# One transformer layer with a mixture of experts on one core: weight pieces on multiples of 512 bytes, two changes of PSUM banks, and a ring of 20 pieces in place of 19

## The chip, the core and the metric

The kernel runs on one core of a Trainium2 chip. The core has a matrix engine (TensorE, PE in the profile), whose matmuls write into 8 banks of PSUM; VectorE (DVE), ScalarE (ACT), GpSimd (POOL) and SyncE (SP), whose queue issues all the transfers here; and 16 DMA engines that bring data from the chip's memory (HBM) into the core's own (SBUF, 128 partitions). The metric is the time of one execution in microseconds. All data are float32.

## What is computed

The reference is one layer for 256 tokens of width 1024: a mixer (differential attention and a gated linear recurrence side by side, from one input projection), and then a mixture of 32 experts of which each token takes 4. Cut to the part that takes most of the time:

```python
def moe(h, router_w, router_b, w_gate_up, b_gate_up, w_down, b_down):
    logits = xf @ router_w + router_b               # 256 tokens x 32 experts
    top_v, top_i = lax.top_k(logits, 4)
    gates = jax.nn.softmax(top_v, axis=-1)
    ...                                             # for the tokens of each expert e:
        gu = xb @ w_gate_up[e] + b_gate_up[e]       # 1024 -> 2 x 1024
        g, u = jnp.split(gu, 2, axis=-1)
        g = jnp.minimum(g, 7.0); u = jnp.clip(u, -7.0, 7.0)
        y = ((u + 1.0) * (g * jax.nn.sigmoid(1.702 * g))) @ w_down[e] + b_down[e]
    ...                                             # out[token] += gate * y
```

An expert has 12 MB (12 x 1.049 MB) of weights; the 32 of them are 403 MB of the 462 MB that the kernel reads.

## The kernel before

**Pieces and the ring.** Weights lie in pieces of 128 partitions x 2048 float32 (8 KB of a partition, 1 MB in all). `piece(i)` (L72) gives piece i: 16 (`NA`) from the pool `arena`, which also serve the mixer, and 3 (`NM`) from the pool `mo`, which takes the room of the mixer's pool `late` after the mixer. In the experts the pieces form a ring, `slots`: `spot()` turns it by one, and `chunk()` (L84, its DMA is L87) loads into the piece that it gives. An expert loads eight pieces of `w_gate_up` (128 rows of 2048 each, an 8 KB row to a partition) and four of `w_down` (two rows of 4 KB to a partition). A load waits until PE has read what lay in its piece before, one whole turn of the ring ago. All loads go through SP's queue in order.

**Pools in SBUF.** `const` lies first, then `arena`, then `small`; `mo` and `late` are laid out from the other end. Where a piece starts follows from the sizes of the tiles that stand before it. Before the change the arena's pieces start 32 bytes past a multiple of 512, the three of `mo` 480 bytes past one.

**Experts.** The loop at L1131 runs over 32 experts in order; their token counts are read into registers, and `tc.If` picks code by the count. An expert with up to 32 tokens runs blocks of 32 (`gate_up_32` L948, `down_32` L975), with 33 to 64 tokens a block of 64 (`gate_up_64` L937, `down_64` L967), and with 65 to 96 both: a block of 64 and one of 32 for the rest (`so`, `gdo`), first the one of 32 and then the one of 64. More than 96 tokens take `rare` (L1072) and `rest_of` (L1026), after the loop's last loads. On PE the order of an expert is: the gate and up matmuls (in two halves of four pieces), a filler (`fill`: the matmuls that gather the tokens of the next pair of experts, `gather` L907), and then `out_of` (L1017) once or twice: `transposed` (L958) turns the activations, `turned` (L992) the combine weights, the down matmuls run over four pieces, ACT copies the result to `y`, and `combine` (L997) multiplies by the weights into four PSUM tiles that DVE adds to `acc` (L1007). Experts go in pairs (`EB` = 2): `gather_batch` (L917) makes one-hot columns on DVE (`onehot`, L892) and then the gathers.

**Banks.** PSUM has the pools `psa` (4 banks), `psb` (2) and `psc` (2); each call of `bank` takes the pool's next one in turn. An expert takes three of `psa` (`pg`, `pu`, `po`). Each `out_of` takes from `psb`: half of the transposes, the down result, two tiles of `combine`; and from `psc`: the other half of the transposes, the bank of `turned`, the other two tiles of `combine`. `gather` takes from `psc`. In `combine` the order of the four tiles is 0, 1, 2, 3 for a block of 32; tiles 0 and 1 are in `psc`, 2 and 3 in `psb`, and DVE adds in the same order.

## Time and profile before

| | us |
|---|---|
| median of three runs (1241.19 to 1246.12) | 1243.11 |
| the profiled execution | 1242.41 |
| its span, first to last instruction | 1240.4 |
| PE busy in the span | 1009.2 (81%) |
| DVE, ACT, POOL busy | 430.8, 227.7, 26.6 |

The profile is one execution of the kernel, recorded instruction by instruction. Its numbers are us from the first instruction on; it has views of busy time by line, of who waited for whom, of stretches of the span ("windows") and of instructions in order of time. "issue" as what ended a wait means that the engine waited for nothing that the profile shows; "PEq" is PE's sequencer; "SPq" is the queue of SyncE, which issues the loads. "PEclk" is the granted clock of TensorE, 1.00 being 2.4 GHz and 0.50 being 1.2 GHz. The DMA engines' mean over the span is 375 GB/s. The mixer takes about the first 270 us, the experts the rest.

### The profile page before, as it was taken

The page shows a single profiled execution, that of the slowest core. Times are in us where ns is not written, and L with a number is a line of the kernel's source. Part 1 is how long each engine was busy: PE and PEld are TensorE (multiplying, and loading weights), DVE is VectorE, ACT ScalarE, POOL GpSimd, SP SyncE. Part 2 cuts the span into 40 slices and gives each one's busy share as a digit, 9 for nine tenths or more (in the row PEclk, how much of TensorE's full clock was granted, in tenths as well). Part 3 has the DMA queues.
Part 4 walks back from the last instruction along what each step waited for, and adds up shares of the span by engine and source line. Part 5 has one row for each costly group of instructions (what it writes and reads, how often), then busy time and mean ns, then how long its engine had stood idle before and what let it go on. Part 6 is the DMA issues. An engine that isn't in the chain of part 4 may idle for free. (4 is left out here: it accounts for less than half of the span.)

```text
span 1240.4 us, 17345 instructions
## 1 busy us (share of the span) xinstructions
PE 1009.2 (81%) x6774; PEld 520.6 (42%) x6774; DVE 430.8 (35%) x843; ACT 227.7 (18%) x426; POOL 26.6 (2%) x36
## 2 busy tenths in 40 slices
PE   6999999998779899888799789668776667787845
PEld 3767777864433333433344333223332222333312
DVE  3498779642222222322222232212222212121212
ACT  3544656331111000100001110000100000010001
POOL 1020100010000000000000000000000000000000
PEclk9999989989999999999999999889989887888978
DMA  9967669879999999799999999999999999999994
GB/s 343 337 242 280 204 215 352 320 319 397 411 413 415 413 415 414 316 391 388 415 413 414 414 413 413 413 415 416 414 413 413 415 412 414 407 407 408 413 411 180
DMA packets 100191, 465.70 MB, mean 375 GB/s; under 512 B 9716, under 2 KB 9814, under 8 KB 67256
## 3 DMA queue, kind: packets, MB, share of 16 engines
q1 hardware_dynamic: 100024, 463.31, 93.7%
q8 instruction: 125, 2.05, 0.7%
q14 instruction: 42, 0.34, 0.1%
HBM read 462.23 MB, written 1.05 MB: 373 GB/s over the span
## 5 line engine op out<-in xcount | busy, mean ns | idle before, releaser
L955 PE MATMUL bank<-piece,xg 128*32 128x512 f32 x1472 | 209.7, 684 | 66.7 <-DMA piece<-in_w_gate_up_dram 54.8
L945 PE MATMUL bank<-piece,xg 128*64 128x512 f32 x768 | 170.7, 596 | 3.6 <-PEq L1155 2.7
L1007 DVE TENSOR_TENSOR acc<-acc,bank 128x512 f32<-128x512 f32 x136 | 84.4, 682 | 249.2 <-PE bank L1004 249.2
L923 DVE TENSOR_SCALAR bank<-bank 128x256 f32<-128x256 f32 (+1 forms) x35 | 18.3, 524 | 373.4 <-PE bank L955 260.4
L955 PEld LDWEIGHTS bank<-piece,xg 128*32 128x32 f32 x1472 | 43.8, 117 | 207.7 <-DMA piece<-in_w_gate_up_dram 123.8
L980 PE MATMUL bank<-piece,actT 128*32 128x256 f32 x1472 | 99.3, 421 | 6.0 <-DMA piece<-in_w_down_dram 2.7
L924 ACT ACTIVATE s<-bank 128x256 f32<-128x256 f32 (+1 forms) x32 | 14.8, 463 | 480.0 <-DVE bank L923 480.0
L945 PEld LDWEIGHTS bank<-piece,xg 128*64 128x64 f32 x768 | 56.1, 138 | 111.5 <-issue 100.5
L913 PEld LDWEIGHTS bank<-oh,x 128*128 128x128 f32 x512 | 87.7, 203 | 31.7 <-issue 22.0
L913 PE MATMUL bank<-oh,x 128*128 128x192 f32 (+1 forms) x512 | 96.8, 346 | 0.4 <-DVE xg L905 0.4
L972 PE MATMUL bank<-piece,actT 128*64 128x512 f32 x384 | 86.5, 604 | 0.8
L130 PE MATMUL bank<-lo,piece 128*128 128x512 f32 x208 | 84.1, 404 | 3.3 <-DVE lo L122 3.3
L131 PE MATMUL bank<-hi,piece 128*128 128x512 f32 x208 | 83.9, 403 | 0.0
L129 PE MATMUL bank<-hi,piece 128*128 128x512 f32 x208 | 82.6, 402 | 0.0
L122 DVE TENSOR_TENSOR lo<-piece,hi 128x1024 fp32r<-128x1024 f32 x60 | 74.0, 1254 | 16.7 <-ACT hi L121 16.5
L980 PEld LDWEIGHTS bank<-piece,actT 128*32 128x32 f32 x1472 | 49.3, 120 | 50.7 <-issue 18.3
L121 ACT CAST hi<-piece 128x1024 fp32r<-128x1024 f32 x60 | 62.0, 1047 | 45.0 <-PE bank L131 36.7
L964 PE MATMUL bank<-ident,s 128*128 128x128 f32 x88 | 17.0, 299 | 63.1 <-DVEq L1188 29.1
L1004 PE MATMUL bank<-y,gt 32*128 32x256 f32 (+1 forms) x544 | 49.2, 396 | 21.0 <-ACT y L1023 21.0
L1004 PEld LDWEIGHTS bank<-y,gt 32*128 32x128 f32 (+1 forms) x544 | 33.4, 185 | 44.2 <-ACT y L1023 42.1
L972 PEld LDWEIGHTS bank<-piece,actT 128*64 128x64 f32 x384 | 26.8, 139 | 52.8 <-issue 48.0
L1023 ACT COPY y<-bank 128x256 f32<-128x256 f32 (+1 forms) x35 | 15.6, 445 | 179.4 <-PE bank L980 96.9
(265 smaller groups left out, 875.2 us busy)
## 6 DMA issues: line engine op xcount, KB each, us to landing
piece<-in_w_gate_up_dram SPq DMA_DIRECT2D x256, 1024.0 KB, 20.2
piece<-in_w_down_dram SPq DMA_DIRECT2D x128, 1024.0 KB, 20.3
piece<-in_w_in_dram SPq DMA_DIRECT2D x22, 1024.0 KB, 6.6
piece<-in_w_mod_dram SPq DMA_DIRECT2D x16, 1024.0 KB, 8.3
piece<-in_w_mod_dram SPq DMA_DIRECT2D x16, 512.0 KB, 7.0
piece<-in_w_out_dram SPq DMA_DIRECT2D x4, 1024.0 KB, 5.1
piece<-in_w_branch_a_dram SPq DMA_DIRECT2D x2, 1024.0 KB, 8.0
piece<-in_w_branch_b_dram SPq DMA_DIRECT2D x2, 1024.0 KB, 7.5
```

Source lines behind the costliest of these rows:

```text
L121: now(A, lambda: nc.scalar.copy(hi, v[:, h]))
L122: now(V, lambda: nc.vector.tensor_tensor(lo, v[:, h], hi.bitcast(F32), ALU.subtract))
L129: nc.tensor.matmul(out, ah, bh, start=start, stop=False, skip_group_check=True)
L130: nc.tensor.matmul(out, ah, bl, start=False, stop=False, skip_group_check=True)
L131: return nc.tensor.matmul(out, al, bh, start=False, stop=stop, skip_group_check=True)
L913: last = nc.tensor.matmul(ph[:, j], x[:, t, k * P : (k + 1) * P], oh[:, t, cs], start=t == 0, stop=t == NT - 1)
L945: nc.tensor.matmul(pp[r : r + C], xg[:, k, :C], wg[k][:, 0, 512 * q : 512 * (q + 1)], start=False, stop=k == KD - 1, skip_group_check=True)
L955: nc.tensor.matmul(halves(po[U * q : U * q + U]), xg[:, k, s0 : s0 + U], quarter(wg[k][:, 0], q), start=False, stop=k == KD - 1, skip_grou ...
L972: nc.tensor.matmul(py[C * n : C * n + C], at[:, j, C * half : C * half + C], wd[kk // 2][:, kk % 2, 512 * n : 512 * (n + 1)], start=kk == ...
L980: nc.tensor.matmul(py[U * c : U * c + U, 0:256], at[:, j, U * q : U * q + U], wd[kk // 2][:, kk % 2, 256 * c : 256 * (c + 1)], start=kk == ...
L1004: nc.tensor.matmul(pcs[c][:, t], gt[r : r + n, t * P : (t + 1) * P], y[r : r + n, w : w + 256], start=True, stop=True)
L1007: nc.vector.tensor_tensor(acc[:, :, cs], acc[:, :, cs], pcs[c], ALU.add)
```

## The change

- `NM` goes from 3 to 4: a fourth piece in `mo`, the ring has 20.
- Room for it: one buffer in place of two for the one-hot tile `oh`; the tile `y` goes (the down result is copied into `so` or into the activations' own tile); `w2` lies in a buffer of `xg` and is made as the filler of expert 30, no longer at expert 27; `xr` of the overflow path lies in a ring piece.
- Places: `iota` has 128 columns in place of 352, `r2` is padded to 96 columns and `gt` by 120, so that all pieces, of the arena and of `mo`, start at multiples of 512 bytes. The overflow path compares with shifted positions (`moved`), since `iota` is shorter.
- Banks: `turned` gets a bank of `psa` in every expert (`pt`), no longer one of `psc`; `combine` of a block of 32 takes its tiles in the order 2, 0, 3, 1.

```diff
--- before.py
+++ after.py
@@ -40,7 +40,7 @@
 EB = 2
 BIG = 3.0e38
 NA = 16
-NM = 3
+NM = 4
 LASTS = 27
 NOSYNC = mybir.DependencyInfo(mybir.DependencyClass.NoSync, mybir.DependencyReason.DATA)
 NEG = float(np.finfo(np.float32).min)
@@ -169,11 +169,11 @@
     lower = late.tile([P, P], F32, name="lower")
     nc.gpsimd.affine_select(out=lower, in_=ones, pattern=[[1, P]], compare_op=ALU.is_gt, fill=0.0,
                             base=0, channel_multiplier=-1)
-    iota = const.tile([P, S + CA], F32, name="iota")
-    nc.gpsimd.iota(iota, pattern=[[1, S + CA]], base=1, channel_multiplier=0, allow_small_or_imprecise_dtypes=True)
+    iota = const.tile([P, P], F32, name="iota")
+    nc.gpsimd.iota(iota, pattern=[[1, P]], base=1, channel_multiplier=0, allow_small_or_imprecise_dtypes=True)
 
     xn2 = part(11, 0, NT, D)
-    r2 = const.tile([P, NT], F32, name="r2")
+    r2 = const.tile([P, 96], F32, name="r2")[:, :NT]
     acc = const.tile([P, NT, D], F32, name="acc")
     gw2 = const.tile([P, KD], F32, name="gw2")
     s2 = late.tile([P, D], F32, name="s2")
@@ -893,7 +893,7 @@
         return last
 
     def onehot(e0, ne, s0, n):
-        oh = mo.tile([P, NT, EB, CA], F32, name="oh")
+        oh = mo.tile([P, NT, EB, CA], F32, name="oh", bufs=1)
         oh = oh.rearrange("p t e c -> p t (e c)")[:, :, : ne * n].rearrange("p t (e c) -> p t e c", c=n)
         for t in range(NT):
             slot_is(oh[:, t], t, e0, ne, s0, n)
@@ -997,7 +997,7 @@
     def combine(gt, y, n):
 
         pcs = [bank((psc, psb)[c // 2], NT, 256) for c in range(4)]
-        order = range(4) if n == U else (0, 2, 1, 3)
+        order = (2, 0, 3, 1) if n == U else (0, 2, 1, 3)
         for t in range(NT):
             for c in order:
                 r, w = (U * c, 0) if n == U else (C * (c // 2), 256 * (c % 2))
@@ -1017,15 +1017,16 @@
     def out_of(at, wd, n, y, gd, gt, fin, pt):
 
         py = bank(psb)
-        turned(gd, gt, bank(psc) if pt is None else pt)
+        turned(gd, gt, pt)
         (down_64 if n == C else down_32)(at, wd, py)
         w = 512 if n == C else 256
         nc.scalar.copy(y[:, :w], py[:, :w])
         combine(gt, y, n) if fin is None else combine_into(fin, gt, y, n)
 
-    def rest_of(e, s0, xr, spare):
-
-        ring = deque(spare[1:])
+    def rest_of(e, s0, spare):
+
+        ring = deque(spare[2:])
+        xr = part(piece(spare[1]), 0, KD, P)
 
         def half(w, kh, n):
 
@@ -1034,7 +1035,11 @@
             nc.sync.dma_start(v, rows(a[w][e], 512 * kh, 4)[:, :, 512 * n : 512 * (n + 1)])
             return v
 
-        oh = onehot(e, 1, s0, P)
+        moved = small.tile([P, NT], F32, name="moved")
+        nc.vector.tensor_scalar(moved, posm[:, :, e], float(-s0), None, ALU.add)
+        oh = mo.tile([P, NT, P], F32, name="oh", bufs=1)
+        for t in range(NT):
+            nc.vector.tensor_scalar(oh[:, t], iota, moved[:, t : t + 1], r2[:, t : t + 1], ALU.is_equal, ALU.mult)
         for kp in range(KD // 2):
             gather(oh, xr, kp, pool=psb)
         p = piece(spare[0])
@@ -1049,11 +1054,11 @@
                     for k in range(4):
                         nc.tensor.matmul(pp[i], xr[:, 4 * kh + k, :P], w[:, k], start=False, stop=kh == 1 and k == 3)
             transposed(swiglu(*pp, s), at[:, h], 4)
-        gd = mo.tile([P, 512], F32, name="y", bufs=1)
+        gd = mo.tile([P, 512], F32, name="s", bufs=1)
         pt = bank(psb, S)
         for t in range(NT):
             gv = gd[:, t * P : (t + 1) * P]
-            weigh(gv.unsqueeze(1), e, t, s0)
+            nc.vector.tensor_scalar(gv, iota, moved[:, t : t + 1], gates[:, t, e : e + 1], ALU.is_equal, ALU.mult)
             nc.tensor.transpose(pt[:, t * P : (t + 1) * P], gv, ident)
         nc.scalar.copy(gt, pt)
         for n in range(2):
@@ -1073,19 +1078,18 @@
 
         engines = [ET.PE, ET.Activation, ET.DVE, ET.SP]
         of = lambda i: nc.values_load(counts[0:1, i : i + 1], engines=engines, min_val=0, max_val=S)
-        xr = mo.tile([P, KD, EB * CA], F32, name="xg")
         with tc.If(of(NE) > CA) as some:
             for e in range(NE):
                 cnt = of(e)
                 with tc.If(cnt > CA):
-                    rest_of(e, CA, xr, spare)
+                    rest_of(e, CA, spare)
                     with tc.If(cnt > CA + P):
-                        rest_of(e, CA + P, xr, spare)
+                        rest_of(e, CA + P, spare)
         return some
 
 
     xg = mo.tile([P, KD, EB * CA], F32, name="xg")
-    oh = mo.tile([P, NT, EB, CA], F32, name="oh")
+    oh = mo.tile([P, NT, EB, CA], F32, name="oh", bufs=1)
     for t in range(NT):
         seq(V, lambda: slot_is(oh[:, t], t, 0, EB, 0, CA))
     count()
@@ -1127,7 +1131,7 @@
 
     down_loads = lambda e: [chunk(rows(a["w_down"][e], 2 * P * i, 2), 2, D) for i in range(4)]
     after = load(0)
-    fin = pt = other = None
+    fin = other = None
     for e in range(NE):
         j = e % EB
         cnt = after
@@ -1135,13 +1139,17 @@
         if e == NE - 1:
             wd = down_loads(e)
             step(rare(list(slots)[: len(slots) - KD - 4]).cond_inst)
-        if e == LASTS:
-            w2 = mo.tile([P, D], F32, name="w2", bufs=1)
-            for n, pr in enumerate(rows_of(gw2, psc)):
-                nc.scalar.copy(w2[:, 512 * n : 512 * (n + 1)], pr)
         if j == 0:
             xgn, todo = gather_batch(e + EB) if e + EB < NE else (None, [])
             fill = first if e == 0 else todo[:2]
+            if e == NE - 2:
+                w2 = mo.tile([P, KD, EB * CA], F32, name="xg").rearrange("p a b -> p (a b)")[:, :D]
+
+                def gated_rows():
+                    for n, pr in enumerate(rows_of(gw2, psc)):
+                        nc.scalar.copy(w2[:, 512 * n : 512 * (n + 1)], pr)
+
+                fill = [gated_rows]
         elif e < NE - 1:
             fill = todo[0 if e == 1 else 2 :] + (down_bias() if e == LASTS else [])
         xe = xg[:, :, j * CA : (j + 1) * CA]
@@ -1182,25 +1190,26 @@
             after = in_turn(lambda: load(e + 1))
             wd = down_loads(e)
         else:
-            pt, other = bank(psa), bank(psa)
+            other = bank(psa)
+        pt = bank(psa)
         at = mo.tile([P, 4, P], F32, name="actT", bufs=1)
-        y, gt = mo.tile([P, 512], F32, name="y", bufs=1), mo.tile([P, S], F32, name="gt", bufs=1)
+        gt = mo.tile([P, S + 120], F32, name="gt", bufs=1)[:, :S]
         with tc.If(cnt > C) as more:
             transposed(so, at[:, 0:2], 2, other)
-            out_of(at[:, 0:2], wd, U, y, gdo, gt, fin, pt)
+            out_of(at[:, 0:2], wd, U, so, gdo, gt, fin, pt)
         step(more.cond_inst)
         with tc.If(cnt > U) as many:
             transposed(act, at, 4, other)
-            out_of(at, wd, C, y, gd, gt, fin, pt)
+            out_of(at, wd, C, act, gd, gt, fin, pt)
         with many.Else():
             transposed(act[:, :256], at[:, 0:2], 2, other)
-            out_of(at[:, 0:2], wd, U, y, gd, gt, fin, pt)
+            out_of(at[:, 0:2], wd, U, act, gd, gt, fin, pt)
         step(many.cond_inst)
         if j == EB - 1:
             xg = xgn
 
 
-    sq = mo.tile([P, NT, 256], BF16, name="fsq", tag="oh")
+    sq = mo.tile([P, NT, 256], BF16, name="fsq", tag="oh", bufs=1)
     ss = small.tile([P, NT, 4], F32, name="fss")
 
     def squares(t, c):
```

## Rows read from the trace of the kernel before

**Rows 1.** the page's slices of the span: GB/s moved in 40 equal slices

```profile
GB/s 343 337 242 280 204 215 352 320 319 397 411 413 415 413 415 414 316 391 388 415 413 414 414 413 413 413 415 416 414 413 413 415 412 414 407 407 408 413 411 180
```

**Rows 2.** waits of the queue that issues loads, whole span: us, times, longest

```profile
SPq L87 <- DMA piece<-in_w_gate_up_dram: 238.1, 133, 3.1
SPq L87 <- DMA piece<-in_w_down_dram: 187.3, 93, 3.0
```

**Rows 3.** DMA issues: name, count, KB each, median us to landing

```profile
piece<-in_w_gate_up_dram SPq DMA_DIRECT2D x256, 1024.0 KB, 20.2
piece<-in_w_out_dram SPq DMA_DIRECT2D x4, 1024.0 KB, 5.1
x<-in_x_dram SPq DMA_DIRECT2D x1, 1024.0 KB, 5.0
```

**Rows 4.** windows: us, busy by engine, PEclk, DMA share, GB/s

```profile
271.00:560.00 289.00, 246.94 (x1680) 108.98 (x1684) 78.32 (x168) 30.94 (x69) 0.00 (x0) 0.98 0.98 396
560.00:1226.00 666.00, 508.95 (x3786) 214.05 (x3782) 156.15 (x340) 58.98 (x140) 0.00 (x0) 0.90 1.01 408
```

**Rows 5.** waits of PE, 271 to 560 us: us, times, longest

```profile
PE bank L964 <- issue: 8.9, 2, 5.0
PE bank L935 <- issue: 4.1, 1, 4.1
PE bank L994 <- DVE xg L905: 2.2, 2, 1.2
PE bank L955 <- DMA piece<-in_w_gate_up_dram: 0.5, 1, 0.5
```

**Rows 6.** waits of PE, 560 to 1230 us

```profile
PE bank L955 <- DMA piece<-in_w_gate_up_dram: 54.3, 50, 2.2
PE bank L964 <- issue: 18.3, 5, 4.8
```

**Rows 7.** windows of 10 us

```profile
260.00:270.00 10.00, 9.14 (x44) 9.00 (x44) 4.44 (x27) 1.79 (x5) 1.80 (x1) 0.50 1.01 421
510.00:520.00 10.00, 7.48 (x48) 3.28 (x50) 2.91 (x5) 1.10 (x3) 0.00 (x0) 1.00 0.42 161
520.00:530.00 10.00, 8.85 (x52) 3.75 (x50) 3.08 (x6) 0.58 (x1) 0.00 (x0) 1.00 0.93 359
560.00:570.00 10.00, 9.49 (x70) 2.78 (x63) 0.43 (x1) 0.32 (x1) 0.00 (x0) 0.81 0.92 329
```

**Rows 8.** waits of the queue in 508 to 535, then 552 to 568 us

```profile
SPq L87 <- PE bank L972: 18.3, 4, 14.4
SPq L87 <- PE bank L955: 12.7, 5, 8.8
```

**Rows 9.** timeline, two experts with over 64 tokens: start, us, engine, line

```profile
459.16 0.26 ACT L965 COPY actT<-bank 128x128 f32<-128x128 f32 x1
459.92 0.41 PE L994 MATMUL bank<-ident,gdo 128*128 128x128 f32 x2 [0.99 <-DVE xg L905]
465.63 2.48 DVE L1007 TENSOR_TENSOR acc<-acc,bank 128x512 f32<-128x512 f32 x4 [5.66 <-PE bank L1004]
467.66 0.63 PE L964 MATMUL bank<-ident,s 128*128 128x128 f32 x4 [2.05 <-DVE acc L1007]
468.61 8.55 PE L972 MATMUL bank<-piece,actT 128*64 128x512 f32 x32
...
514.52 7.09 PE L972 MATMUL bank<-piece,actT 128*64 128x512 f32 x32
```

**Rows 10.** window in the first of these experts

```profile
468.00:472.00 4.00, 4.00 (x15) 1.44 (x15) 0.53 (x2) 0.74 (x2) 0.00 (x0) 0.57 1.03 413
```

**Rows 11.** timeline of PE: first matmuls of two experts

```profile
558.60 0.62 PE L935 MATMUL bank<-bgu,sel 96*32 96x512 bf16 x4 [4.14 <-issue]
...
1208.25 0.62 PE L935 MATMUL bank<-bgu,sel 96*32 96x512 bf16 x4 [6.68 <-PEq L1155]
```

**Rows 12.** groups of instructions by line: count, busy us, mean ns, idle before

```profile
L892 DVE TENSOR_SCALAR oh<-iota,posm,r 128x96 f32<-128x96 f32 x64 | 18.1, 324 | 3.7 <-PE bank L913 2.0 <-DVE xg L905 0.8
```

## The prediction, made before the result was known

> **What bounds the kernel now.** I read the slices of the span first: the DMA engines move 407 to 416 GB/s nearly everywhere after the first quarter, with one hole near 500 to 560 us [rows 1]. The queue that issues the loads mostly waits for earlier loads: 238.1 and 187.3 us [rows 2]. A load of 1024 KB (1.049 MB) takes 1.049/0.413 = 2.54 us of transfer and lands 20.2 us after its issue [rows 3], so some eight are under way at a time; a deeper ring does not make the transfer itself quicker.
>
> Then I split the expert stage in two, because the hole does. From 271 to 560 us PE is busy 246.94 of 289 us and the rate is 396; from 560 to 1226 us PE is busy 508.95 of 666 and the rate is 408 [rows 4]. PE's own waits say the same more sharply. In the first stretch it waited for a load 0.5 us in all; the rest is its own idle time ("issue"), DVE's banks and ACT [rows 5]. In the second it waited 54.3 us for loads [rows 6]. So **PE sets the time up to about 560 us, and the loads set it from there to the end.** The places where the loads stood still are 510 to 530 and 560 to 570 us: against 414 GB/s the three windows shown lose (414-161)/41.4 = 6.1, 1.3 and 2.1 us, 9.5 us together [rows 7]. There the queue waited for a ring piece that PE still read: up to 14.4 us for the down matmuls at L972, then up to 8.8 us for the gate matmuls at L955 [rows 8]. The second of these is the joint: that expert's first matmul came at 558.60, after 4.14 us of idle time [rows 11], and what follows it is transfer to the end.
>
> Hence the measure of the change: how much earlier the load goes out that hangs on this expert, plus any change of rate in the 666 us behind it. Loss in transfers earlier than that is worth nothing by itself.
>
> **The 20th piece.** Twelve loads an expert go round the ring; load n waits for PE to finish load n minus 19. With 20, the load that had to wait for the expert beginning at 558.60 is the following one, so everything behind is one transfer ahead: 2.5 us. It is also worth 2.5 us at 516 us, but PE in between does not wait for loads [rows 5], so the two don't add. Ends: 0, if PE falls back by as much, and 5.0, if PE turned out to be fed late in between. I take 2.5. The queue gains no load, only another piece in its cycle; before the experts one more load is issued, into time that PE then sets.
>
> **The bank changes.** They matter in experts with over 64 tokens, which run two blocks one behind the other. Two of these lie in PE's stretch (about 434 to 525 us). First, `turned` moves from a psc bank to a psa bank of its own: today its transposes wait for DVE to empty the second gather bank, 2.2 us in two waits [rows 5], 0.99 of it before the row at 459.92 [rows 9]. Without it the down matmuls behind (L980, at 460.26) wait for ACT's copy of the transposed activations alone, which ends at 459.42 [rows 9]: 0.8 us earlier, and the same in the other expert, 1.6 us. Second, `combine` of the 32-slot block goes through its banks as 2, 0, 3, 1, and DVE adds them in that order. Today the transposes of the second block wait 2.05 us behind the adds, which take 2.48 us for four, 0.62 each: the psb bank that they need first is the third [rows 9]. In the new order it is the first and the psc bank is the second. The first pair may start at 0.62, the second pair at 1.24; with the pair and `turned` behind it the down matmuls start about 1.0 us earlier. Two experts: 2.0 us. DVE's copy of the second half now queues behind two remaining adds and ends about where it does now; the down matmuls reach it only after a quarter of their 7.09 us, so that is covered.
>
> A third effect may come with it: in the first of these experts the down matmuls took 8.55 us, in the next 7.09 [rows 9], because the granted clock was 0.57 over 468 to 472 us [rows 10] (mostly its lower level, 1.2 GHz) after a stretch of waits on PE. Shorter waits may spare the 1.46 us; the next expert, with the same waits, kept full speed. Ends 0 and 1.46, I take half, 0.7. The banks together: 1.6 + 2.0 + 0.7 = 4.3 us, between 1.2 (the two waits of 2.05 shortened by one add each, no more) and 5.1.
>
> The price of the bank: psa now hands out four banks an expert, so the gate's bank is the one of the expert before. Its reader, the swiglu, is over before PE's transposes of that expert start; no wait.
>
> **The alignment.** iota loses 896 bytes of a partition and r2 gains 352, which moves the 16 arena pieces from 32 past a multiple of 512 onto it; the ring's own pieces move from 480 past. No aligned piece is in the trace. Nearest rows: x, at 128 past, lands 5.0 us after its issue, a w_out load at 32 past 5.1 us [rows 3], with other row lengths. The best 10 us with unaligned pieces reached 421 GB/s, when 8 KB rows alone were on the way [rows 7]; against 408 [rows 4] no more than 666 x 13/421 = 20 us are to be had. A slice of 31 us holds one to three of the 480 pieces among twelve, and slices differ by a few GB/s [rows 1], too little to tell the two starts apart. I take 0, nearest to the two landings, and keep 0 to -20 as bounds, the slow side excluded because a start on a multiple can't split a row into more parts.
>
> What the Trainium skill says stands apart from this sum. Its page "DMA: Bandwidth & Descriptors", section "How a descriptor splits into AXI transactions", lets a transfer that starts off a 256-byte boundary pay for the bytes below its start, in beats of 32 bytes. By its figures, an estimate: one beat more in 256 for an 8 KB row at 32 past, seven at 480 past, about 1% over the ring's mix, some 7 us of 666. That page speaks of reads; no row here shows it for writes into SBUF.
>
> **What I cost at nothing.** One one-hot buffer in place of two: its writer (0.324 us an instruction [rows 12], four a batch) now waits for the gathers of the batch before, which end an expert earlier, except in the first expert, where the write moves behind its four gathers: 0 to 1.3 us on DVE, with an expert's time until its result is read. `so` and the activations as `y`: the next writer is the next expert's swiglu, a whole gate later. w2 moves from expert 27 to expert 30 as a filler, a few us of PE; PE then has 6.68 us of idle time before 1208.25 [rows 11]. If that cover were gone, up to 3 us at the end. The overflow path (`rest_of`) isn't run; paddings and the small iota cost nothing.
>
> **The sum.** 2.5 + 4.3 + 0 = 6.8 us. The profiled execution took 1242.41 us (span 1240.4 and 2.0 around it), 0.7 below the median of 1243.11; the loss or gain is the same for both: 1243.1 - 6.8 = 1236.3 us.
>
> **Rivals.**
> 1. *Given back before the joint.* PE's idle time "issue" is 8.9 us in two waits and 4.1 in one from 271 to 560 [rows 5]; if a part of it ends at a fixed event rather than after PE's work, an earlier arrival is waited out there. So too if the ring's load merely waits behind its eighth predecessor. Gain 0 to 3: 1240 to 1243, centre 1241.5. For it: the joint itself is such a wait. Chance 0.22.
> 2. *The placement does change the rate of transfer.* A third of the bound is 7 us, half is 10: 1236.3 - 7 to 10 = 1226 to 1229. For it: the diff moves every piece. Against it: two landings within 0.1 us [rows 3]. The Trainium skill's rule quoted above would give 1229. Chance 0.15.
> 3. *Slower: the idle time moves.* The stalls "issue" of 4 to 5 us fall between blocks: three up to 560 us [rows 5], five more at the transposes after it [rows 6], hidden behind the loads. The change alters PE's instruction stream in every expert; if the places shift and more of them fall before 560, each costs its full 4.2 us. One or two eat the gain; from the third on the kernel is slower: 1236.3 + 3 x 4.2 = 1249. Chance 0.1.
> 4. *It does not do what it says:* the pieces come to lie elsewhere, or the ring's order leaves the new piece late. Then only the banks remain: 1243.1 - 4.3 = 1238.8. Chance 0.08.
>
> The forecast itself has 0.45, with 1231 to 1241 as its own range.
>
> **How the numbers follow.** A measurement of this kernel can tell about 0.5% (6.2 us) from no change, so faster means below 1236.9. Of the forecast somewhat over half lies there, with all of rival 2: 0.27 + 0.15, and a little for both at once, 0.48 in all. Slower by as much needs rival 3 in full, or something not seen: 0.11. The rest, 0.41, is within. The range takes in rival 2 and the milder end of rival 3 and leaves out about 0.2: 1226 to 1247.
>
> **What would show it.** Right: the windows from 510 to 530 and 560 to 570 us near 400 GB/s, the wait of L964 for DVE's adds near 0.7 us, none of L994 for the gather, and the end earlier by what the joint is earlier. Alignment at work: the rate from there to the end above 408 by more than 2, and landing below 20 us. Wrong: more "issue" time on PE before the joint, or a new wait of DVE for PE ahead of the one-hot.

## The result, and the profile after

| | before | after |
|---|---|---|
| median, us (lowest to highest) | 1242.15 (1240.05 to 1246.12) | 1225.65 (1223.11 to 1227.75) |
| the profiled execution, us | 1242.41 | 1223.11 |
| its span, us | 1240.4 | 1221.1 |

The ratio of after to before is 0.9863, 95% interval 0.9829 to 0.9896: faster by 1.4%, some 17 us. The forecast was 1236.3 us in a range from 1226 to 1247. The gain is two and a half times the one forecast, and the time lies just under the range, at the lower edge of rival 2 (1226 to 1229).

The slices of the page of after (GB/s in 40 equal slices), beside [rows 1]:

```profile
GB/s 349 363 228 281 207 203 364 310 346 399 410 421 422 422 424 422 329 400 386 423 421 423 422 422 422 422 422 424 422 422 422 423 422 422 418 413 422 419 418 146
```

In the experts 413 to 416 has become 421 to 424. The hole in slices 17 to 19 is still there. The issues (name, count, KB each, median us to landing), beside 20.2 in [rows 3], say the same, with nothing changed in what is loaded:

```profile
piece<-in_w_gate_up_dram SPq DMA_DIRECT2D x256, 1024.0 KB, 19.6
piece<-in_w_down_dram SPq DMA_DIRECT2D x128, 1024.0 KB, 19.6
```

The windows up to the joint and behind it (us, busy time of PE, PEld, DVE, ACT, POOL, PEclk, DMA share, GB/s), beside [rows 4]:

```profile
271.00:556.00 285.00, 247.01 (x1676) 108.96 (x1676) 76.33 (x163) 29.51 (x67) 0.00 (x0) 0.98 0.98 404
556.00:1205.00 649.00, 499.64 (x3762) 213.05 (x3758) 156.53 (x344) 59.01 (x140) 0.00 (x0) 0.92 1.00 416
```

Both rates rose by 8 GB/s, 2%. PE's busy time in the first window is what it was: PE still sets the time there. The places where the loads stood still (windows of 10 us, columns as above), beside [rows 7], lost as much as before:

```profile
505.00:515.00 10.00, 8.46 (x62) 4.42 (x56) 2.81 (x5) 1.12 (x3) 0.00 (x0) 1.00 0.39 156
515.00:525.00 10.00, 8.98 (x52) 3.85 (x50) 3.08 (x6) 0.59 (x1) 0.00 (x0) 1.00 1.00 383
555.00:565.00 10.00, 9.49 (x65) 3.44 (x58) 0.43 (x1) 0.19 (x1) 0.00 (x0) 0.81 0.83 326
```

PE's waits (us in total, times, longest), beside [rows 5]; the first row is of 271 to 556 us, the second of 440 to 530 us:

```profile
PE bank L964 <- issue: 8.6, 2, 4.6
...
PE bank L964 <- DVE acc L1007: 2.1, 4, 0.9
```

The second row in before, 440 to 535 us:

```profile
PE bank L964 <- DVE acc L1007: 4.1, 2, 2.0
```

The two long waits for DVE's adds have become short ones, and the wait of L994 for the gather is gone from the list, as the prediction had it. The joint and the last expert's start (timeline of PE), beside [rows 11]:

```profile
553.11 0.62 PE L935 MATMUL bank<-bgu,sel 96*32 96x512 bf16 x4 [4.02 <-issue]
...
1186.61 0.62 PE L935 MATMUL bank<-bgu,sel 96*32 96x512 bf16 x4 [6.33 <-DVEq L1081]
```

The joint came 5.5 us earlier, the last expert 21.6 us. So most of the gain arose behind the joint, in the transfers. Cut at four events, the profiled execution of every kernel of this study reads as follows (us; "stage" is from the first expert's first matmul to the joint; the last landing of a weight piece and of an output are read from the transfers' records; another 1.0 us to the end of the span):

| kernel | first expert | stage | joint to last weight landing | to last output landing | span |
|---|---|---|---|---|---|
| before | 271.3 | 287.3 | 668.5 | 12.3 | 1240.4 |
| after | 269.2 | 283.9 | 652.6 | 14.5 | 1221.1 |
| e1, before, aligned only | 268.6 | 287.2 | 654.8 | 12.3 | 1223.9 |
| e2, after, pieces at 32 and 480 | 271.7 | 285.8 | 666.5 | 15.6 | 1240.6 |
| e3, after, pieces at 256 | 268.8 | 283.6 | 652.7 | 14.5 | 1220.7 |
| e4, after, pieces at 128 | 271.1 | 286.6 | 664.1 | 14.2 | 1237.0 |
| e11, after, pieces at 64 | 269.9 | 286.5 | 665.1 | 13.3 | 1235.7 |
| e7, after, four pieces at 480 | 268.6 | 284.2 | 653.8 | 15.8 | 1223.4 |
| e5, after, old banks | 271.9 | 290.0 | 652.7 | 13.8 | 1229.4 |
| e6, after, 19 pieces | 268.5 | 284.2 | 654.7 | 14.8 | 1223.2 |
| e8, after, 8 KB rows for w_down | 268.5 | 283.8 | 649.6 | 16.7 | 1219.6 |
| e9, e8 with TensorE's code moved | 268.7 | 280.6 | 650.8 | 12.7 | 1213.8 |
| e10, e8 with it moved twice as far | 271.4 | 282.9 | 650.1 | 14.7 | 1220.0 |

Each row is one execution, and not every column is equally firm. The third stretch repeats within 0.1 us where it should (652.6, 652.7 and 652.7 in after, e3 and e5). The first does not: six kernels with all pieces at multiples of 256 came to the first expert at 268.5 to 269.2 us, two others (e5, e10) at 271.9 and 271.4, as late as before. The stage moves by one to three microseconds with the granted clock.

### The profile page after: what moved, and what is told of

Its sections match the earlier page's. It is cut to its first block, busy times and chain, and to the rows that moved or that the text cites. A ratio compares the mean times of both kernels' runs of the same rounds, so it can differ in the third digit from the quotient of the medians.

```text
span 1221.1 us, 17353 instructions
## 1 busy us (share of the span) xinstructions
PE 1002.5 (82%) x6774; PEld 520.9 (43%) x6774; DVE 430.0 (35%) x843; ACT 227.5 (19%) x426; POOL 26.5 (2%) x36
## 3 DMA queue, kind: packets, MB, share of 16 engines
q8 instruction: 125, 2.05, 0.6%
## 5 line engine op out<-in xcount | busy, mean ns | idle before, releaser
L955 PE MATMUL bank<-piece,xg 128*32 128x512 f32 x1472 | 199.1, 656 | 62.8 <-DMA piece<-in_w_gate_up_dram 49.9
L980 PE MATMUL bank<-piece,actT 128*32 128x256 f32 x1472 | 107.4, 445 | 5.9 <-issue 2.3
L913 PEld LDWEIGHTS bank<-oh,x 128*128 128x128 f32 x512 | 85.4, 198 | 29.5 <-issue 19.6
L122 DVE TENSOR_TENSOR lo<-piece,hi 128x1024 fp32r<-128x1024 f32 x60 | 73.9, 1253 | 16.3 <-ACT hi L121 16.2
L980 PEld LDWEIGHTS bank<-piece,actT 128*32 128x32 f32 x1472 | 53.0, 127 | 55.2 <-issue 24.2
L964 PE MATMUL bank<-ident,s 128*128 128x128 f32 x88 | 17.4, 298 | 62.6 <-issue 30.1
L1004 PE MATMUL bank<-s,gt 32*128 32x256 f32 (+1 forms) x496 | 45.7, 396 | 17.5 <-ACT s L1023 17.5
L1004 PEld LDWEIGHTS bank<-s,gt 32*128 32x128 f32 (+1 forms) x496 | 31.3, 185 | 39.3 <-ACT s L1023 37.2
L1023 ACT COPY s<-bank 128x256 f32<-128x256 f32 (+1 forms) x32 | 14.5, 453 | 173.9 <-PE bank L980 91.7
## 6 DMA issues: line engine op xcount, KB each, us to landing
piece<-in_w_gate_up_dram SPq DMA_DIRECT2D x256, 1024.0 KB, 19.6
piece<-in_w_down_dram SPq DMA_DIRECT2D x128, 1024.0 KB, 19.6
```

The costliest lines, as they stand in the source:

```text
L122: now(V, lambda: nc.vector.tensor_tensor(lo, v[:, h], hi.bitcast(F32), ALU.subtract))
L913: last = nc.tensor.matmul(ph[:, j], x[:, t, k * P : (k + 1) * P], oh[:, t, cs], start=t == 0, stop=t == NT - 1)
L955: nc.tensor.matmul(halves(po[U * q : U * q + U]), xg[:, k, s0 : s0 + U], quarter(wg[k][:, 0], q), start=False, stop=k == KD - 1, skip_grou ...
L980: nc.tensor.matmul(py[U * c : U * c + U, 0:256], at[:, j, U * q : U * q + U], wd[kk // 2][:, kk % 2, 256 * c : 256 * (c + 1)], start=kk == ...
L1004: nc.tensor.matmul(pcs[c][:, t], gt[r : r + n, t * P : (t + 1) * P], y[r : r + n, w : w + 256], start=True, stop=True)
```

## Experiments

The ratio given with each time is to runs of the kernel before that were made beside it; their median was 1244.86 us for e1 to e4, 1243.24 for e5 to e8 and 1245.11 for e9 to e11.

### Is it the place of the pieces? (e1, e2)

e1 is the kernel before with two paddings and nothing else; the paddings put all its 19 pieces at multiples of 512 bytes.

```
-    iota = const.tile([P, S + CA], F32, name="iota")
+    iota = const.tile([P, S + CA + 120], F32, name="iota")[:, : S + CA]
...
-        y, gt = mo.tile([P, 512], F32, name="y", bufs=1), mo.tile([P, S], F32, name="gt", bufs=1)
+        y, gt = mo.tile([P, 512], F32, name="y", bufs=1), mo.tile([P, S + 120], F32, name="gt", bufs=1)[:, :S]
```

> The kernel before with two paddings alone (120 columns behind iota, 120 behind gt): all 19 pieces start at multiples of 512 bytes, ring of 19 and banks as before. Theory A (the places of the pieces shorten every transfer): between 600 and 1000 us the rate is 422 GB/s as in the changed kernel in place of 414, loads land about 19.6 us after their issue in place of 20.2, the joint (first matmul of the expert that began at 558.60) moves by the 2 us of the mixer alone, and the time is 1242 - 2 - 12 = 1228 us. Theory B (the rate rose because PE, DVE or the ring ask differently): 414 GB/s, 20.2 us, 1242 us.

Measured: 1226.67 us, 0.9869 of before (0.9838 to 0.99). e2 is the kernel after with the paddings chosen so that the pieces lie again where they lay before.

```
-    r2 = const.tile([P, 96], F32, name="r2")[:, :NT]
+    r2 = const.tile([P, 104], F32, name="r2")[:, :NT]
...
-        gt = mo.tile([P, S + 120], F32, name="gt", bufs=1)[:, :S]
+        gt = mo.tile([P, S + 128], F32, name="gt", bufs=1)[:, :S]
```

> The changed kernel with its pieces shifted back off the multiples: the arena's 32 bytes past, the ring's own four 480 past; ring of 20 and banks as changed. Theory A: 414 GB/s between 600 and 1000 us; what is left of the gain is the joint (about 4 us) and one transfer (2.5): 1242 - 6.5 = 1235.5 us. Theory B: 422 GB/s and 1226 us.

Measured: 1242.18 us, 0.9968 of before (0.9946 to 0.999). The rate of the two (windows from the joint to the last loads, e1 first, then e2):

```profile
558.00:1210.00 652.00, 500.27 (x3798) 212.96 (x3790) 155.92 (x340) 58.99 (x140) 0.00 (x0) 0.92 1.00 416
```

```profile
560.00:1222.00 662.00, 508.83 (x3742) 213.32 (x3734) 156.38 (x343) 58.38 (x138) 0.00 (x0) 0.90 1.01 408
```

416 with aligned pieces and 408 without, whichever kernel it is. So the padding alone makes nearly all of the gain, and theory A holds. But e2 missed its own number by 6.7 us: the other parts, worth 6.5 by the expectation, showed as 0.3% of the time. Where their part went is the question of e5, e6 and e9.

### Which boundary? (e3, e4, e11)

The same edit with other numbers: all pieces 256, 128 or 64 bytes past a multiple of 512.

> The changed kernel with every piece 256 bytes past a multiple of 512. If it is a boundary of 256 bytes that counts: as the changed kernel, 422 GB/s and 1226 us. If it is 512: as with 32 and 480 past, 414 GB/s and 1235.5 us.

> The changed kernel with every piece 128 bytes past a multiple of 512. If a boundary of 256 or 512 bytes counts: 414 GB/s and 1235.5 us, as with 32 and 480 past. If 128 bytes or less are enough, and 32 is the fault: 422 GB/s and 1226 us.

> The kernel after with all 20 pieces at 64 bytes past a multiple of 512. Measured so far: 0 and 256 past give 1224.9 to 1225.7 us, 128 past 1238.0 us, 32 and 480 past 1242.2 us. Theory A, what counts is only whether a piece starts at a multiple of 256 bytes: as 128 past, 1238 us, 415 GB/s in the slices of the experts. Theory B, the loss grows as the common divisor with 256 falls: between 1238 and 1242 us.

Measured: at 256, 1224.95 us, 0.985 of before (0.9823 to 0.9878); at 128, 1238.01 us, 0.995 (0.993 to 0.9971); at 64, one time, 1237.64 us beside 1245.11 for the kernel before. The slices of the three pages, in this order:

```profile
GB/s 351 357 235 279 207 208 363 311 344 403 408 420 423 422 424 423 329 406 380 423 421 423 422 421 423 422 421 423 423 422 421 422 422 423 416 413 422 421 419 144
```

```profile
GB/s 337 341 257 273 201 201 360 332 339 391 407 415 416 415 417 416 342 405 365 416 415 415 415 415 415 415 416 417 415 415 415 415 415 413 409 404 415 414 412 148
```

```profile
GB/s 340 343 254 276 198 207 359 328 347 396 412 414 416 414 416 415 336 395 374 416 415 415 414 414 415 414 415 417 415 414 413 416 413 416 405 407 411 412 408 168
```

256 is as good as 0 (421 to 424), 128 and 64 are nearly as bad as 32 and 480 (414 to 417). Of e11's two theories the first is the nearer: a multiple of 256 counts, and how far off it the piece starts counts for little. e11 is one execution, and the intervals of e2 and e4 overlap, so a small difference between the places is not excluded.

### Does each piece pay for itself? (e7)

Only the four pieces of the pool `mo` go to 480 past a multiple, by a padding of `gt` of 128 columns in place of 120.

> The kernel after with only the 4 ring pieces of the mixed pool moved to 480 bytes past a multiple of 512; the other 16 stay at multiples. Theory A, each transfer bears the place of its own piece: a fifth of the loads is slower, by some 0.06 us each, so that a fifth of the 16.5 us between all pieces aligned and all pieces off (1225.7 and 1242.2 us) is lost: 1229.0 us, and the landing gaps of those four pieces are 2.50 us where the others have 2.44. Theory B, one queue shares the loss (packets of different pieces stand in the same engines, a slow one holds the next up): more than a fifth, up to all of it, 1229 to 1242 us, with longer gaps on all pieces. Theory C, only the large arena's pieces matter: 1225.7 us.

Measured: 1224.91 us, 0.9851 of before (0.982 to 0.9881): no loss that the times show, which by itself would be theory C. By the profile the stretch from the joint to the last weight landing is 1.2 us longer than in after, where a fifth of the 13.9 us between after and e2 would be 2.8. The records of the single packets between 600 and 1190 us tell more. Of the 8 KB packets 98.9% took 309 ns in after; in before 10% did, 51% took 313 and 16% 320. In e7, with a fifth of the pieces off the boundary, 93.6% still took 309. The slow ones stand together once in each turn of the ring, where the four pieces are filled: nine tenths of them within seven of its twenty loads. So these pieces do pay, against theory C; but only some three in ten of the packets into them were slow (an estimate from these counts), where with all pieces off the boundary nine in ten are. None of the three theories foresaw that: at a fifth of the pieces the loss is less than a fifth.

A start off the boundary is therefore not enough to make a packet slow. Before shows the same in the 10 us from 260 us on [rows 7]: every piece lay off the boundary there, the DMA engines were fully busy (share 1.01), and 68% of the 8 KB packets still took 309 ns. What has to come with it was not tried.

### Banks and ring on top of the alignment (e5, e6)

e5 undoes the two bank changes in after (`pt` is None but in the last expert, as in before):

```
-        order = (2, 0, 3, 1) if n == U else (0, 2, 1, 3)
+        order = range(4) if n == U else (0, 2, 1, 3)
...
-        turned(gd, gt, pt)
+        turned(gd, gt, bank(psc) if pt is None else pt)
...
-            other = bank(psa)
-        pt = bank(psa)
+            pt, other = bank(psa), bank(psa)
```

e6 goes back to 19 pieces (aligned):

```
-NM = 4
+NM = 3
```

> The kernel after, with its two bank changes undone: the turned mask goes to a psc bank again and the combine of 32-slot experts runs in the order 0, 1, 2, 3. In the trace of after, the stage from 558 us of before (the joint: the first matmul of the expert that began at 558.60 us) stands 2.7 us earlier than in the aligned-only kernel (553.1 against 555.8 us). Theory A, the banks gave those 2.7 us: the joint goes back to about 555.8 us and the time to 1228.4 us. Theory B, the stage catches up whatever the banks do, because its clock or its transfers take back what the banks give: the joint stays within 1 us of 553.1 and the time stays at 1225.7 us. Further: after its last weight piece lands, after takes 11.7 us to the last output's landing, the kernel before 9.5. If the banks cause that, this kernel goes back to 9.5 us, and the time by this alone falls by 2.2 us.

> The kernel after with 19 ring pieces instead of 20, all still at multiples of 512 bytes. Theory A, the 20th piece is worth one landing gap of an aligned transfer (2.45 us), since the transfers run without a break from the joint to the end: 1228.1 us, with the last weight piece landing 2.45 us later against the joint. Theory B, what lies behind the last landing takes it back (the tail grew from 9.5 to 11.7 us between before and after): the tail shrinks to 9.5 us and the time stays at 1225.7 us.

Measured: 1229.41 us, 0.9874 of before (0.9851 to 0.9898), and 1229.0 us, 0.988 (0.9857 to 0.9902). These intervals and that of after (0.9829 to 0.9896) overlap, so the times can't place parts of 2 to 3 us; the medians lean to theory A in both. The table of stretches can. Undoing the ring piece lengthens the third stretch from 652.6 to 654.7 us, by 2.1. Undoing the banks lengthens the stage from 283.9 to 290.0 us; 2.7 of these 6.1 us are the clock's: of the six groups of down matmuls over 64 slots ahead of the joint three took 8.1 to 8.8 us in e5 and one in after, against 7.09 at full clock. e1, with one such group (8.69), has the old banks' stage at 287.2.

The last stretch answers the second question of e5 (the expectations of e5 and e6 count it 2.8 us shorter, 9.5 and 11.7 where the table has 12.3 and 14.5). It is 12.3 us in before and e1, 13.8 with old banks and 20 pieces, 14.8 with new banks and 19 pieces, 14.5 in after. So the kernel with the new banks alone has the whole of the growth, the one with the ring alone 1.5 of the 2.2 us, and the two do not add. The timelines of PE in the last expert, of before and then of after, show how:

```profile
1218.14 3.70 PE L1176 MATMUL bank<-acc,ident 128*128 128x512 f32 x8
1222.41 0.41 PE L964 MATMUL bank<-ident,s 128*128 128x128 f32 x2 [0.57 <-PEq L1188]
1222.66 0.38 PE L994 MATMUL bank<-ident,gd 128*128 128x128 f32 x2
1224.44 3.75 PE L980 MATMUL bank<-piece,actT 128*32 128x256 f32 x64 [1.40 <-ACT gt L995]
```

```profile
1197.00 3.70 PE L1184 MATMUL bank<-acc,ident 128*128 128x512 f32 x8
1202.98 0.41 PE L964 MATMUL bank<-ident,s 128*128 128x128 f32 x2 [2.28 <-issue]
1203.23 0.38 PE L994 MATMUL bank<-ident,gd 128*128 128x128 f32 x2
1203.64 5.35 PE L980 MATMUL bank<-piece,actT 128*32 128x256 f32 x64
```

In before PE waited 0.57 us ahead of the transposes; in after 2.28, for nothing that the profile shows. After that the down matmuls ran 1.6 us longer, at a granted clock of 0.68 (partly at the lower level, 1.2 GHz) where before it was 1.00 (windows of these matmuls, before and then after, columns as above):

```profile
1224.40:1228.20 3.80, 3.75 (x64) 2.14 (x63) 0.00 (x0) 0.00 (x0) 0.00 (x0) 1.00 0.20 79
```

```profile
1203.60:1209.00 5.40, 5.36 (x65) 2.67 (x64) 0.12 (x1) 0.37 (x1) 0.00 (x0) 0.68 0.03 11
```

The psa bank did remove the 1.40 us that L980 waited for `turned`'s copy. The last weight piece landed at 1205.7 us in after, and PE finished with it only at 1209.0; in before it landed at 1227.1 and PE was done at 1228.2. So with after's pieces the end of the kernel hangs on PE again. In the kernels with new banks and unmoved code (e2, e3, e4, e6, e7, e11) the same wait is 2.0 to 2.5 us, in e1 and e5 0.57 and 0.56.

### What "issue" is (e8, e9, e10)

e8 is the candidate that the landing gaps pointed to: in after a `w_down` load (two rows of 4 KB to a partition) landed 2.474 us after its predecessor, a `gate_up` load (one row of 8 KB) 2.439 (medians). The three calls of `transposed` in the expert loop pass `pairs` as True:

```
-    down_loads = lambda e: [chunk(rows(a["w_down"][e], 2 * P * i, 2), 2, D) for i in range(4)]
+    down_loads = lambda e: [chunk(a["w_down"][e][2 * P * i : 2 * P * (i + 1), :].rearrange("(p k) n -> p k n", k=2), 2, D) for i in range(4)]
...
-                nc.tensor.transpose(pt[:, j], act[:, (m * i + j) * P : (m * i + j + 1) * P], ident)
+                b = m * i + j
+                cols = slice(256 * (b // 2) + b % 2, 256 * (b // 2 + 1), 2) if pairs else slice(b * P, (b + 1) * P)
+                nc.tensor.transpose(pt[:, j], act[:, cols], ident)
```

> The kernel after, with each w_down piece loaded so that a partition takes two neighbouring rows of 4 KB, one packet of 8 KB instead of two of 4 KB; the transposes of the activations read every second column to match. In after, a gate_up load (8 KB packets, all aligned) lands 2.439 us after the one before it and a w_down load (4 KB packets) 2.474 us after it. Theory A, the difference is the price of the second packet's start: w_down's gap falls to 2.44 us, 88 of its loads lie behind the joint, 88 x 0.035 = 3.1 us, 1222.6 us. Theory B, the difference has another cause (what else moves while w_down loads): the gap stays at 2.474 us and the time at 1225.7 us. Theory C, the reads of every second column make the transposes longer and the gain is given back there: gap 2.44 us, the transposes ahead of the down matmuls longer than 0.41 to 0.66 us.

Measured: 1221.55 us, 0.9827 of before (0.9801 to 0.9853). The gap fell to 2.440 us, the third stretch by 3.0 us, as theory A says; but the last stretch grew from 14.5 to 16.7 us, since PE is the later one there by more. Its waits of PE for "issue" stand where those of after stand. That gave the next test: e9 and e10 put 32 and 64 one-column matmuls ahead of the first transposes, where PE waits for the first transfer anyway. The profiles of e9 and e10 have 127 and 255 instructions more than that of e8.

```
+    for i in range(32):
+        nc.tensor.matmul(pt[0:1, 0:1], ident[0:KD, 0:1], ident[0:KD, 1:2], start=True, stop=True)
     nc.tensor.transpose(pt, crow, ident[0:KD, 0:KD])
```

> The kernel with 8 KB packets for w_down, and 32 matmuls of one column put ahead of the first transposes, in the 6 us in which TensorE waits for its first transfer: they move all later TensorE code by some 128 instructions and do nothing else (their result is overwritten). Question: in the last expert, after the four matmuls that start the final sums, TensorE is idle for 2.0 to 2.5 us in the kernels with the new bank changes and for 0.57 us in those without; an instruction packet of 16 KB is in flight there in all of them. Theory A, the idle time is a wait for code and hangs on where in the code the branch stands: it changes with the shift, to about 0.6 us, or turns up elsewhere; if it goes, the last d32 also runs at a higher clock and the stretch from the last weight landing to the last output landing falls from 16.7 us to 13 to 14.5 us, the time from 1221.6 to about 1219 us. Theory B, the new banks themselves cause it: 2.0 to 2.5 us as before, 1221.6 us.

> As the run before, with 64 such matmuls, some 256 instructions, about one packet of code. Theory A: the idle time ahead of the last expert's transposes again depends on the place; with a shift of a whole packet it may be as without a shift (2.0 to 2.5 us), and 1221.6 us. Theory B: 2.0 to 2.5 us in all three, so that this run alone does not tell them apart; the pair does.

Measured: 1219.7 us, 0.9798 of before (0.9764 to 0.9832), and 1223.11 us, 0.9836 (0.9793 to 0.9878). PE in the last expert of e9 (timeline):

```profile
1194.81 1.88 PE L1188 MATMUL bank<-acc,ident 128*128 128x512 f32 x4
1197.27 0.47 PE L968 MATMUL bank<-ident,s 128*128 128x128 f32 x2 [0.58 <-PEq L1201]
1197.58 0.38 PE L998 MATMUL bank<-ident,gd 128*128 128x128 f32 x2
1197.98 3.66 PE L984 MATMUL bank<-piece,actT 128*32 128x256 f32 x64
```

The idle time is 0.58 us and the down matmuls run at full clock again. The same transposes in e8 and e10:

```profile
1201.36 0.48 PE L966 MATMUL bank<-ident,s 128*128 128x128 f32 x2 [2.35 <-issue]
```

```profile
1201.94 0.48 PE L968 MATMUL bank<-ident,s 128*128 128x128 f32 x2 [2.02 <-issue]
```

And the joint in e8, e9 and e10:

```profile
552.32 0.62 PE L935 MATMUL bank<-bgu,sel 96*32 96x512 bf16 x4 [3.86 <-issue]
```

```profile
549.29 0.40 PE L937 MATMUL bank<-bgu,sel 96*32 96x512 bf16 x4 [0.50 <-PEq L1167]
```

```profile
554.23 0.62 PE L937 MATMUL bank<-bgu,sel 96*32 96x512 bf16 x4 [4.18 <-issue]
```

The waits ahead of the transposes in the first three experts are 1.58, 4.58, 1.26 us in e8, 1.58, 1.44, 4.01 in e9 and 1.57, 4.76, 1.26 in e10. PE's waits for "issue" from 271 us to shortly before the joint (us in total, times, longest; the longest rows only) in e8, e9 and e10:

```profile
PE bank L966 <- issue: 8.4, 2, 4.6
```

```profile
PE bank L937 <- issue: 4.1, 1, 4.1
PE bank L968 <- issue: 4.0, 1, 4.0
```

```profile
PE bank L968 <- issue: 8.8, 2, 4.8
```

So the long idle times called "issue" hang on where TensorE's code stands: a shift by some 128 instructions moves them, one by some 256 brings them back to their places. The packets of the queue that brings instructions (16 KB each, 125 in after) say the same directly. From 271 us on PE was idle for 3.5 to 5 us 8 times in before, 10 times in after and 6 times in e9, and every one of these times ended 1.4 to 1.7 us after such a packet had come in; so did the 2.28 us in the last expert of after (1.6). Theory A holds, and the new banks are not the cause by themselves, since e9 has them too. They come with 28 more instructions on TensorE's sequencer (526 records against 498 in before, e1 and e5), which fits; code with the old banks was not moved. How many instructions one packet holds no run shows.

By the medians e9 is faster than after by 0.65% (0.9798 against 0.9863), but the intervals still touch (up to 0.9832, down to 0.9829). By its median it is the fastest kernel of the study, 2% below before (its interval reaches to 0.9832).

## Why the prediction was wrong, point by point

**What bounds the kernel: right.** PE sets the time to the joint, and the loads from there. The joint is again an expert that begins after 4.0 us of "issue", and behind it the loads don't break off.

**The 20th piece, 2.5 us: right in kind, 2.1 measured** (652.6 in after against 654.7 in e6; 666.5 in e2 against 668.5 in before). It is one transfer, as worked out.

**The banks, 4.3 us: 3.3 measured** (287.2 in e1 to 283.9 in after). The two waits went as worked out: L994's for the gather is gone, L964's for DVE's adds fell from 2.05 to 0.85 us, in the two experts of [rows 9]. In their place came 0.9 us of short waits of L980 for the copies of the activations. What was mis-sized is the clock, 0.7 us: the slow down matmuls of [rows 9] did become quick, but others became slow instead, one expert earlier (the first row of after; the second is the expert of [rows 9]):

```profile
422.10 8.78 PE L972 MATMUL bank<-piece,actT 128*64 128x512 f32 x32
466.32 7.09 PE L972 MATMUL bank<-piece,actT 128*64 128x512 f32 x32
```

Before, these took 7.09 and 8.55. In the other kernels, too, one such group is slow as a rule, in changing experts (none in e6 and e10). Without the clock's term the sum for the banks was 3.6. Where pieces are off the boundary the stage gained only 1.5 us (287.3 to 285.8 in e2) or 0.7 (e4). Some 1 us of the difference is the clock's: the time below full clock in the stage, weighted by how far below, adds up to 5.9 us in before, 5.7 in after, 6.9 in e2 and 7.3 in e4. The rest was not settled.

**The alignment, 0: the step that failed.** It is worth 13.7 us behind the joint in e1 (668.5 to 654.8) and 13.9 between e2 and after (666.5 to 652.6); e1's ratio gives 16.3 us in all. In e1 the first expert also began 2.7 us earlier (271.3 to 268.6), but that this is the alignment's is not shown: e5 and e10, with aligned pieces, began as late as before. I took 0 for the nearest rows, x at 128 past and a `w_out` load at 32 past, which land 5.0 and 5.1 us after their issue [rows 3]. But e4 shows that 128 past is itself a bad place. The two rows compared two slow starts and said nothing about an aligned one. Moreover those are landing times of loads that go alone or nearly so, and the loss is one of the rate at full use: in after the same `w_out` loads land 4.9 us after their issue, while the experts' loads went from 20.2 to 19.6. The row that did speak was beside them, and I read it as a mere bound: the 10 us in which 8 KB rows came at 421 GB/s with pieces off the boundary [rows 7]. That is the rate at which after runs for 600 us, and in these 10 us 68% of the 8 KB packets were as quick as in after. The bound of 0 to -20 held the truth; "nearest to the two landings" picked the wrong end of it. Rival 2, which set the lower end of the range, was priced at a third to a half of the 20 us; two thirds came, and so the time fell out of the range.

The Trainium skill, page "DMA: Bandwidth & Descriptors", section "How a descriptor splits into AXI transactions", has a boundary of 256 bytes, and e3 and e4 agree with it: 256 past is as good as 0, 128 is not. The page says it of reads; here the off-boundary side is what is written in SBUF. In size they differ. By its beats my estimate was 1%, and the rate moved by 2% (408 to 416). By its beats, again an estimate, a start at 128 past would cost four beats a row, one at 32 past one and one at 480 past seven, for e2 some two on average, and e4 (0.995) is not slower than e2 (0.9968). The measurement decides.

**The end, 0: wrong by 2.2 us, the other way** (12.3 to 14.5). I had costed everything behind the last load as unchanged. It is not the quicker transfers as such: e1 has them and keeps 12.3. Part comes with the 20th piece, since PE then finishes with the last piece later behind its landing (2.7 us in e5, which has the old banks, 1.1 in before and e1); part is the "issue" of 2.28 us and the lower clock after it, as e9 shows, which is without it at 12.7. That is the mechanism of rival 3 (the idle time moves), in one place and not three; and it is why e2, with ring and banks alone, kept 0.3% and not the 6.5 us that I expected of it: 1.5 us in the stage and 2.0 behind it, less 3.3 at the end and 0.4 in the mixer. Its one profile shows nothing left of them; its ratio 4 us.

**What was costed at nothing** held. PE still stood idle for 6.33 us before the last expert, which covered the moved `w2`; DVE's waits ahead of the one-hot for the gathers stayed at 2.0 us in all.

**The rivals.** Rival 1 (given back before the joint) did not come true: the stage kept its 3.3 us. Something was given back, but behind the last landing. Rival 4 fell with e1 to e4, which act as the places worked out from their paddings say, and with e6: the new piece is not late. Rival 2 decided. In sum, from the table's rows of before and after: 2.1 up to the first expert, 3.4 in the stage and 15.9 behind the joint (rate and ring), less 2.2 at the end, are 19.2 of the 19.3 us by which the span fell. The medians fell by 16.5: the profiled execution of after is the fastest of its four.

## What to carry to other kernels

Where loads set the time, look at the address of every buffer that they fill: here two paddings of 480 bytes a partition gave what the remaining edits together did not. A row is evidence for "no effect" only if one of its sides lies in the state that the change brings about; two slow cases that agree prove nothing, and a rate reached once, for ten microseconds, is a reason to ask what keeps it from lasting. When the transfers get quicker, look again at what ends last behind them, and take idle time that the profile can't explain as possibly a matter of where the code lies: set its end beside the packets that bring instructions.

## What the runs showed of the hardware

- Weight pieces whose partition rows start off a multiple of 256 bytes in SBUF cost 2% of the rate over 650 us of full use (408 against 416 GB/s; with pieces 32 and 480 past, 8 KB packets mostly 313 to 320 ns against 309, 4 KB packets 160 to 166 against 159). A multiple of 256 is enough; with all pieces at 64, at 128, or at 32 and 480 past, it is slow.
- The loss is not proportional, and the start alone does not make a packet slow: with a fifth of the pieces off the boundary 93.6% of the 8 KB packets took 309 ns, and from 260 to 270 us of before, with all of them off, 68%.
- Two packets of 4 KB cost 0.034 us a load of 1 MB more than one of 8 KB (2.474 against 2.440 us between landings).
- TensorE's idle times of 2 to 5 us that end by nothing in the profile move when its code moves: some 128 instructions more took the one at the end from 2.35 to 0.58 us and the joint's from 3.86 to 0.50 us (the stage fell from 283.8 to 280.6 us); some 256 more brought both back, to 2.02 and 4.18 us. Those of 3.5 to 5 us in before, after and e9 end 1.4 to 1.7 us after a 16 KB packet of the instruction queue has come in. That the engine waits for its code follows from the two together; how much code it waits for is not shown.
